# Four mixer layers on one core: softmax weights normalised on GpSimd before their transposes, and in the second layer GpSimd also makes low halves and ends rotations

## Chip, cores, metric

One core of one Trainium2 chip runs the whole program in one launch. The metric is the device time of one execution, in microseconds (us). The engines of the core are PE (TensorE, matmuls and transposes through the array; PEld is its weight load), DVE (VectorE), ACT (ScalarE), POOL (GpSimd) and SP (SyncE, which issues nearly all DMAs). PSUM is what PE writes to; DVE and ACT read and write it too.

## What is computed

A block with retention, mLSTM and a feed-forward part (`first_block`), and behind it four layers, whose mixers are dense attention, windowed attention with sinks, a long convolution, and dense attention again. The first and the fourth (8 heads, queries of 128 plus 64 rotated dimensions, 256 context keys and 512 own keys):

```python
def dense_attend(q, k, v, scale):
    s = jnp.einsum('bqhd,bkhd->bhqk', q, k).astype(jnp.float32) * scale
    p = jax.nn.softmax(s, axis=-1).astype(v.dtype)
    return jnp.einsum('bhqk,bkhd->bqhd', p, v)
```

The second has 16 query heads on 4 key heads of 64 dimensions; each query block of 128 sees up to three key blocks around it and the 256 context keys, and a sink, one learned score per head that enters the softmax and has no value row:

```python
def sink_attend(scores, values, sink_l):
    sink_col = jnp.broadcast_to(sink_l[None, :, :, None, None], scores[0].shape[:-1] + (1,))
    p = jax.nn.softmax(jnp.concatenate(scores + [sink_col], axis=-1), axis=-1)
...
```

Each attention output is multiplied by `silu(gate)` and goes through an output matrix. The third mixer needs filters `h @ f_w3` times an exponential decay for its convolution, and the kernel makes them early, beside the feed-forward part.

## The kernel before

All arithmetic is float32. To use PE's fast float32 format, every factor of a large product is split: the high half is the value rounded to that format (ACT, a copy), the low half what the rounding left (DVE, value minus high half). `split` (lines 396 to 398) does it. A product is three matmuls per 128 rows of depth, high by high, high by low and low by high (`mac`, lines 441 to 443). PE therefore has most of the work.

Weights come by DMA as `raw` tiles of 128x1024 (four buffers) and are split into `whi` and `wlo` (three of each, `wslot`) by `wm`, or into tiles that are held longer by `wheld` (`P` or `b` tiles). The stages are written as Python generators, and `mix` and `weave` interleave their steps, so that projections of the next heads lie between the attention steps of the present ones. From that the build makes one fixed list of instructions for each engine, and each engine works off its list in order; nothing overtakes.

Dense attention (`mla`): `prep` makes queries, keys and values of a pair of heads; its rotated query parts go through `rope64` (four ACT copies of 32 partitions in `swap32`, then line 1356 times cosine, 1357 times sine, 1358 the sum, all DVE) and `stacks`, which puts high and low half of 64 rows above each other. `stageA` makes the scores of 128 queries in PSUM (lines 1581 to 1583 and `mac`), and `softmax` makes the weights `P`: the largest score of each row (line 1380, DVE), times minus the scale (1382, DVE), the exponential with its row sum (1385, ACT), and 1 over the sum into a column of `rd` (1389, DVE). `P` stays unnormalised. `stageB` turns each block of 128 keys of the four (context: two) `P` tiles round on PE (`transposed`, line 1395), splits them out of PSUM, and multiplies with V. Only at the end it normalises: `over_columns` (line 1373) spreads the `rd` columns over all partitions by one PE transpose each, the gate `g` is multiplied with that (1605) and with the output (1606).

Windowed attention (`swa`): a unit is 128 queries of one key head with its four query heads; there are 24, of 256, 512 or 640 keys. `stageA` of one unit is mixed with `stageB` of the one before (`attend`). `softmax` gets the sink: the row maximum is held against it (1384), the sink's exponential (1387, ACT) is added to the sum (1388, DVE). In `stageB`, V is laid out as high half (64 columns) and low half (64 columns) of one stationary tile, `v[:, g]`, so that line 1739 gives two partial outputs on 128 partitions, and line 1738 or 1741 adds high half by low weights on 64 of them. Then `over_columns` again, ACT moves that to SBUF (1744), DVE multiplies (1745), adds the two halves (1749) and gates (1752).

Filters (`filter_head`, `filter_unit`): the hidden activations stand as high half (64 rows) over low half (64 rows) in `self.fh`; line 1873 multiplies 128 rows, line 1874 the upper 64 rows with the low halves of the filter weights. This is done 48 times.

Each normalisation of activations takes the power -0.5 of its sums on POOL (line 245, tile `rs`), which is spread by `over_columns` too. Otherwise POOL has little to do outside the third layer (lines 1995, 1996).

Of the kernel before, what the change touches and what calls it, by code (L numbers as in the profile page):

```python
# [19 lines left out]
N = 512  # L20
# [234 lines left out]
class Kern:  # L255
    def __init__(self, tc, I, coff, dbg=None):
        self.tc, self.nc, self.I, self.coff = tc, tc.nc, I, coff
        self.dbg = dbg or {}
        self.st = ExitStack()

# [135 lines left out]
    def split(self, dst, src):  # L396
        self.nc.scalar.copy(dst.hi, src)  # L397
        self.nc.vector.tensor_tensor(dst.lo, src, dst.hi.bitcast(F32), ALU.subtract)  # L398
# [12 lines left out]
    def wm(self, W, r0, kt, c0, n=128):  # L411

        t = self.wslot(kt, n)
        self.split(t, self.wload(W, r0, kt, c0, n))
        return [t[:, k, :] for k in range(kt)]

    def wheld(self, W, c0, slot, r0=0, kt=KT):
# [6 lines left out]
        for k in range(0, kt, per):  # L424
# [3 lines left out]
            self.split(t, raw[:, k:k + n, :])  # L428
# [932 lines left out]
    def stacks(self, r, n, d0, d1):  # L1361

        nc = self.nc
        nc.scalar.copy(d0[0:64, :], r[0:64, :])
        nc.vector.tensor_tensor(d0[64:128, :], r[0:64, :], d0[0:64, :].bitcast(F32), ALU.subtract)
        nc.scalar.copy(d1[64:128, :], r[64:128, :])
        nc.vector.tensor_tensor(d1[0:64, :], r[64:128, :], d1[64:128, :].bitcast(F32), ALU.subtract)
# [8 lines left out]
    def softmax(self, S, P, rd, scale, sink=None):  # L1376

        nc = self.nc
        s = self.sp.tile([128, 8], F32, tag="sm", name="sm")
        nc.vector.tensor_reduce(s[:, 0:1], S, AX.X, ALU.max)  # L1380
        if sink is None:
            nc.vector.tensor_scalar(s[:, 1:2], s[:, 0:1], -scale, None, ALU.mult)  # L1382
        else:
            nc.vector.tensor_scalar(s[:, 1:2], s[:, 0:1], -scale, sink[1], ALU.mult, ALU.min)
        nc.scalar.activation(P, S, AF.Exp, bias=s[:, 1:2], scale=scale, accum_out=s[:, 2:3])  # L1385
        if sink is not None:
            nc.scalar.activation(s[:, 3:4], sink[0], AF.Exp, bias=s[:, 1:2])
            nc.vector.tensor_tensor(s[:, 2:3], s[:, 2:3], s[:, 3:4], ALU.add)
        nc.vector.reciprocal(rd, s[:, 2:3])
# [716 lines left out]
```

## Time and profile before

| | |
|---|---|
| median of 3 runs | 2917.35 us (2915.61 to 2918.12) |
| the profiled execution | 2918.76 us |
| its span, first to last instruction | 2917.0 us |
| PE busy (matmuls) | 2787.1 us, 96% |
| DVE / ACT / POOL busy | 1814.9 (62%) / 1334.4 (46%) / 128.8 us (4%) |
| PE clock granted, mean | 0.982 of full speed |

PE's busy share counts a matmul from its start to a modelled end, and consecutive ones overlap, so the distance from one start to the next is the better measure of what a matmul takes. DVE is at 50 to 80% in most stretches. The stages follow one another: the first block to about 1295 us (the filters from 653 to 1005), the first layer's attention to about 1510, the second layer's from 1650 to 1990, the third layer to about 2500, the fourth layer's attention from 2678 to 2845.

### The profile page before, as it was taken

How to read it: one execution, taken by the hardware profiler on the slowest of the kernel's cores; microseconds unless marked ns; L12 is line 12 of the kernel's file. 1: busy time of each engine (PE TensorE's matmuls, PEld its weight loads, DVE VectorE, ACT ScalarE, POOL GpSimd, SP SyncE). 2: the span in 40 equal slices, each digit the busy share in tenths (PEclk: the TensorE clock that was granted, in tenths of full speed). 3: DMA queues.
4: the chain of work that ended last, by engine and by line, in shares of the span. 5: the costliest groups of instructions: out<-in, count | busy, mean ns of one | idle time of the engine just before them, and what ended most of it. 6: DMA issues, size and time to landing. Idle time of an engine off the chain costs nothing. (4 is left out here: it accounts for less than half of the span.)

```text
span 2917.0 us, 44103 instructions
## 1 busy us (share of the span) xinstructions
PE 2787.1 (96%) x17106; PEld 2364.2 (81%) x17106; DVE 1814.9 (62%) x3775; ACT 1334.4 (46%) x2610; POOL 128.8 (4%) x158
## 2 busy tenths in 40 slices
PE   7999999999999999999999999989999998999998
PEld 4888878887777787888889877778888886887887
DVE  6665455555655556246768577788576777754774
ACT  4344344346455433345555566675332223544553
POOL 1000000000000000000000000000021122000000
PEclk8999999999999999999999999999999999999998
DMA  7233232544555536321234241123132226432122
GB/s 264 86 111 123 73 101 84 168 154 141 164 158 163 170 112 209 108 67 44 68 93 156 64 131 42 35 71 117 62 95 84 84 80 195 130 97 63 56 82 69
DMA packets 365830, 318.98 MB, mean 109 GB/s; under 512 B 17511, under 2 KB 326517, under 8 KB 365620
## 3 DMA queue, kind: packets, MB, share of 16 engines
q1 hardware_dynamic: 365204, 315.99, 35.2%
q8 instruction: 134, 2.20, 0.3%
q14 instruction: 76, 0.62, 0.1%
q0 software_dynamic: 416, 0.17, 0.0%
HBM read 273.90 MB, written 42.21 MB: 108 GB/s over the span
## 5 line engine op out<-in xcount | busy, mean ns | idle before, releaser
L441 PE MATMUL mm<-b,whi 128*128 128x512 f32 (+1 forms) x2548 | 895.8, 352 | 4.7 <-ACT whi L397 2.5
L443 PE MATMUL mm<-b,wlo 128*128 128x512 f32 (+1 forms) x2548 | 887.3, 348 | 1.2 <-DVE wlo L398 1.1
L442 PE MATMUL mm<-b,whi 128*128 128x512 f32 (+1 forms) x2548 | 887.6, 348 | 0.0
L441 PEld LDWEIGHTS mm<-b,whi 128*128 128x128 f32 x2548 | 486.1, 191 | 74.4 <-issue 5.8
L443 PEld LDWEIGHTS mm<-b,wlo 128*128 128x128 f32 x2548 | 486.1, 191 | 62.0 <-DVE wlo L398 2.3
L442 PEld LDWEIGHTS mm<-b,whi 128*128 128x128 f32 x2548 | 486.5, 191 | 60.2 <-issue 0.8
L398 DVE TENSOR_TENSOR wlo<-raw,whi 128x1024 fp32r<-128x1024 f32 (+3 forms) x286 | 292.0, 1023 | 239.7 <-ACT whi L397 224.1
L397 ACT CAST whi<-raw 128x1024 fp32r<-128x1024 f32 (+3 forms) x286 | 252.3, 885 | 397.1 <-PE mm L442 253.9
L443 PE MATMUL mm<-b 128*128 128x256 f32 (+1 forms) x628 | 189.4, 302 | 0.5 <-DVE b L398 0.3
L1385 ACT ACTIVATE P<-mm,sm 128x768 f32<-128x768 f32 (+3 forms) x176 | 127.9, 727 | 116.6 <-DVE sm L1382 68.4
L441 PE MATMUL mm<-b 128*128 128x256 f32 (+1 forms) x500 | 158.2, 318 | 8.4 <-ACT P L1385 4.6
L441 PE MATMUL mm<-b,P 128*128 128x256 f32 x560 | 161.8, 289 | 4.0 <-ACT b L575 2.8
L442 PE MATMUL mm<-b,P 128*128 128x256 f32 x560 | 160.4, 286 | 0.9 <-DVE b L576 0.8
L442 PE MATMUL mm<-b 128*128 128x256 f32 (+1 forms) x500 | 153.0, 307 | 0.4 <-DVE b L398 0.3
L1380 DVE TENSOR_REDUCE sm<-mm 128x1 f32<-128x768 f32 (+3 forms) x176 | 128.6, 733 | 39.7 <-PE mm L1583 23.8
L245 POOL TENSOR_TENSOR rs<-rs,mhalf 128x2 f32<-128x2 f32 (+1 forms) x44 | 42.3, 962 | 2427.2 <-DVE rs L244 2279.8
L398 DVE TENSOR_TENSOR t<-mm,t 128x512 fp32r<-128x512 f32 (+1 forms) x208 | 136.5, 663 | 15.3 <-ACT t L397 14.1
L397 ACT CAST t<-mm 128x512 fp32r<-128x512 f32 (+1 forms) x208 | 116.0, 569 | 54.8 <-PE mm L1395 51.6
L235 DVE TENSOR_TENSOR t<-t 128x256 f32<-128x256 f32 (+1 forms) x216 | 92.5, 441 | 71.9 <-ACT t L231 69.4
L1395 PE MATMUL mm<-ct,P 128*128 128x128 f32 x768 | 122.8, 276 | 13.0 <-ACT P L1385 8.2
L231 ACT ACTIVATE t<-b 128x256 f32<-128x256 f32 (+1 forms) x252 | 100.7, 431 | 67.7 <-DVE b L1101 40.9
L443 PEld LDWEIGHTS mm<-b 128*128 128x128 f32 x628 | 120.6, 192 | 5.6 <-DVE b L398 1.3
(351 smaller groups left out, 5129.7 us busy)
## 6 DMA issues: line engine op xcount, KB each, us to landing
raw<-in_w_mod_dram SPq DMA_DIRECT2D x96, 512.0 KB, 4.4
raw<-in_w_ada_dram SPq DMA_DIRECT2D x48, 512.0 KB, 3.9
raw<-in_w_in_dram SPq DMA_DIRECT2D x48, 512.0 KB, 4.0
raw<-in_w_ffn_in_dram SPq DMA_DIRECT2D x44, 512.0 KB, 4.1
raw<-in_c_w_in_dram SPq DMA_DIRECT2D x32, 512.0 KB, 4.3
raw<-in_a_w_in_dram SPq DMA_DIRECT2D x28, 512.0 KB, 4.1
ks<-t SPq DMA_DIRECT2D x48, 256.0 KB, 2.8
raw<-ks SPq DMA_DIRECT2D x24, 512.0 KB, 3.3
```

Of the source, the lines that this page charges most:

```text
L231: self.k.nc.scalar.activation(sq, x, AF.Square)
L235: self.k.nc.vector.tensor_tensor(self.acc, self.acc, sq, ALU.add)
L245: nc.gpsimd.tensor_tensor(s[:, 4:4 + nt], s[:, :nt], self.k.mhalf[:, :nt], ALU.pow)
L397: self.nc.scalar.copy(dst.hi, src)
L398: self.nc.vector.tensor_tensor(dst.lo, src, dst.hi.bitcast(F32), ALU.subtract)
L441: nc.tensor.matmul(ps, l.hi, r.hi, start=start and i == 0, stop=False)
L442: nc.tensor.matmul(ps, l.hi, r.lo, start=False, stop=False)
L443: nc.tensor.matmul(ps, l.lo, r.hi, start=False, stop=stop and i == n - 1)
L1380: nc.vector.tensor_reduce(s[:, 0:1], S, AX.X, ALU.max)
L1385: nc.scalar.activation(P, S, AF.Exp, bias=s[:, 1:2], scale=scale, accum_out=s[:, 2:3])
L1395: self.nc.tensor.transpose(ps[:, 128 * i:128 * i + 128], b, self.ident)
```

## The change

The scale now goes into the queries when they are split. `softmax` takes the negated maximum in one DVE instruction, the exponential, 1 over the sum, and then POOL multiplies the `P` tile by it in place, before the transposes. With that the `over_columns` of `rd`, the multiplication of `g` (1605), and lines 1744 and 1745 go. In the second layer the sink is copied by ACT into the PSUM column behind the scores, so that maximum, exponential and sum take it in, and lines 1384, 1387, 1388 go; ACT copies the lower half of the output (64 partitions) to SBUF before the halves are added; the factor 0.5 moves to the gating; the low weights meet all 128 columns of `v[:, g]`, always behind the high ones. In the second layer (`self.low = nc.gpsimd`) the low halves of weights and the last two steps of a rotation go to POOL. In the filters the second matmul takes all 128 rows, with zeros (POOL memset, 8 times) under the low weights.

```diff
+    def split(self, dst, src, scale=None, low=None):
+        nc = self.nc
+        if scale is None:
+            nc.scalar.copy(dst.hi, src)
+            (low or nc.vector).tensor_tensor(dst.lo, src, dst.hi.bitcast(F32), ALU.subtract)
+        else:
+            nc.scalar.activation(dst.hi, src, AF.Copy, scale=scale)
+            nc.vector.scalar_tensor_tensor(dst.lo, src, scale, dst.hi.bitcast(F32), ALU.mult, ALU.subtract)
...
-        self.split(t, self.wload(W, r0, kt, c0, n))
+        self.split(t, self.wload(W, r0, kt, c0, n), low=self.low)
...
+        low = self.low or nc.vector
         nc.vector.tensor_tensor(a, ps, self.cs["ac"], ALU.mult)
-        nc.vector.tensor_tensor(sw, sw, self.cs["as"], ALU.mult)
-        nc.vector.tensor_tensor(a, a, sw, ALU.add)
+        low.tensor_tensor(sw, sw, self.cs["as"], ALU.mult)
+        low.tensor_tensor(a, a, sw, ALU.add)
...
-    def softmax(self, S, P, rd, scale, sink=None):
+    def softmax(self, S, P, keep):
...
+        s = self.sp.tile([128, 4], F32, tag="sm", name="sm")
+        nc.vector.tensor_reduce(s[:, 0:1], S, AX.X, ALU.max, negate=True)
+        nc.scalar.activation(P, S, AF.Exp, bias=s[:, 0:1], accum_out=s[:, 1:2])
+        nc.vector.reciprocal(s[:, 2:3], s[:, 1:2])
+        nc.gpsimd.tensor_scalar(P[:, :keep], P[:, :keep], s[:, 2:3], None, ALU.mult)
...
-            rd = o["rd", i]
-            nc.vector.tensor_tensor(g, self.over_columns([rd[:, x:x + 1] for x in range(n // 128)], 128), g, ALU.mult)
             nc.vector.tensor_tensor(g, out, g, ALU.mult)
...
+                nc.scalar.copy(ps[:, 768:769], self.sink[:, h:h + 1])
...
-                P = self.P(nb + 256)
-                h = 4 * g + v
-                self.softmax(ps[:, 512 - nb:768], P, rd[:, v:v + 1], scale, (self.sink[:, h:h + 1], nsink[:, h:h + 1]))
+                P = self.P(nb + 257)
+                self.softmax(ps[:, 512 - nb:769], P, nb + 256)
...
-                    last = z == nb + LS - 1
-                    if last:
-                        nc.tensor.matmul(out[:64, :], v[:, g, 0], p.lo, start=False, stop=False)
-                    nc.tensor.matmul(out, v[:, g], p.hi, start=z == LS, stop=last)
-                    if not last:
-                        nc.tensor.matmul(out[:64, :], v[:, g, 0], p.lo, start=False, stop=False)
+                    nc.tensor.matmul(out, v[:, g], p.hi, start=z == LS, stop=False)
+                    nc.tensor.matmul(out, v[:, g], p.lo, start=False, stop=z == nb + LS - 1)
...
-            nc.scalar.activation(rb, self.over_columns([rd[:, x:x + 1] for x in range(4)], 128), AF.Copy, scale=0.5)
-            nc.vector.tensor_tensor(rb, out, rb, ALU.mult)
+            nc.scalar.copy(rb[64:128, :], out[64:128, :])
...
+            nc.gpsimd.memset(l[64:128, :].bitcast(F32), 0.0)
...
-                        nc.tensor.matmul(ps, x[0:64, :], l, start=False, stop=True)
+                        nc.tensor.matmul(ps, x, l, start=False, stop=True)
```

What moves in the engines' lists, at two places. First PE's list in the first layer, where the first unit's weights `P` are turned round (line 1395 before, 1393 now; `mm2` are score tiles, `mm_11970` and `mm_11976` a gate projection). Before:

```order
L1583 MATMUL mm2_11908<-b_10189,b_11555 128x512
L1395 MATMUL mm_11928<-ct_98,P_11868 128x128
L1395 MATMUL mm_11928<-ct_98,P_11885 128x128
L441 MATMUL mm_11970<-b_11243,whi_11962 128x512
L442 MATMUL mm_11970<-b_11244,whi_11962 128x512
L1395 MATMUL mm_11928<-ct_98,P_11902 128x128
L441 MATMUL mm2_11938<-b_11767,b_11641 128x256
```

Now:

```order
L1393 MATMUL mm_11935<-ct_98,P_11892 128x128
L447 MATMUL mm_11976<-b_11251,whi_11968 128x512
L447 MATMUL mm2_11944<-b_11775,b_11649 128x256
L448 MATMUL mm2_11944<-b_11775,b_11649 128x256
L449 MATMUL mm2_11944<-b_11775,b_11650 128x256
L1580 MATMUL mm2_11944<-b_10198,b_11564 128x256
L1581 MATMUL mm2_11944<-b_10198,b_11564 128x256
L447 MATMUL mm2_11944<-b_11764,b_11649 128x512
L448 MATMUL mm2_11944<-b_11765,b_11649 128x512
L449 MATMUL mm2_11944<-b_11764,b_11650 128x512
L1580 MATMUL mm2_11944<-b_10196,b_11564 128x512
L1393 MATMUL mm_11935<-ct_98,P_11909 128x128
```

Between the second and the third tile's transposes there were 2 matmuls and are now 10: the next score tile went ahead of the third transpose.

Second, POOL's list where the first layer ends and the second begins. Before, it holds only the powers of the normalisations there (`rs`):

```order
L245 TENSOR_TENSOR rs_15009<-rs_15009,mhalf_114 128x2
L245 TENSOR_TENSOR rs_15181<-rs_15181,mhalf_114 128x2
L245 TENSOR_TENSOR rs_15347<-rs_15347,mhalf_114 128x2
L245 TENSOR_TENSOR rs_15548<-rs_15548,mhalf_114 128x2
L245 TENSOR_TENSOR rs_20114<-rs_20114,mhalf_114 128x2
```

Now, from the power that was `rs_15009`:

```order
L245 TENSOR_TENSOR rs_14921<-rs_14921,mhalf_114 128x2
L401 TENSOR_TENSOR wlo_15245<-raw_15246,whi_15244 128x1024
L401 TENSOR_TENSOR wlo_15644<-raw_15645,whi_15643 128x1024
L401 TENSOR_TENSOR P_15227<-raw_15224,P_15226 128x512
L401 TENSOR_TENSOR wlo_15650<-raw_15651,whi_15649 128x1024
L401 TENSOR_TENSOR P_15231<-raw_15224,P_15230 128x512
L401 TENSOR_TENSOR P_15237<-raw_15234,P_15236 128x512
L245 TENSOR_TENSOR rs_15093<-rs_15093,mhalf_114 128x2
L401 TENSOR_TENSOR P_15241<-raw_15234,P_15240 128x512
L245 TENSOR_TENSOR rs_15257<-rs_15257,mhalf_114 128x2
L245 TENSOR_TENSOR rs_15458<-rs_15458,mhalf_114 128x2
L1364 TENSOR_TENSOR t_15592<-t_15592,b_15220 128x512
```

Six low halves of the second layer's weights now stand ahead of the power `rs_15093`, and 176 multiplications of `P` (line 1387) and 20 rotation steps (1364, 1365) are added further along, among the low halves that follow.

## Rows read from the trace of the kernel before

**Rows 1.** Stages: us, busy (count) of PE, PEld, DVE, ACT, POOL, then clock, DMA.

```profile
640.00:1005.00 365.00, 365.00 (x1702) 276.04 (x1701) 202.32 (x298) 192.38 (x260) 0.00 (x0) 1.00 0.51 158
1300.00:1510.00 210.00, 201.94 (x1231) 173.92 (x1230) 144.11 (x324) 115.01 (x250) 0.00 (x0) 0.98 0.21 63
1650.00:1990.00 340.00, 309.61 (x1980) 259.00 (x1979) 261.53 (x713) 217.11 (x538) 0.00 (x0) 0.97 0.23 70
2678.00:2845.00 167.00, 162.43 (x926) 137.36 (x927) 115.36 (x226) 95.22 (x188) 0.00 (x0) 0.98 0.21 64
```

**Rows 2.** Groups by line, whole span: busy us, mean ns | idle before, releaser.

```profile
L1373 PE MATMUL mm<-ct,rd 128*128 128x128 f32 x176 | 28.6, 279 | 0.0
...
L1874 PEld LDWEIGHTS mm<-b 64*128 64x128 f32 x48 | 9.1, 190 | 14.6 <-issue 14.6
```

**Rows 3.** Timeline of PE at 1537 us: start, duration, line.

```profile
1537.45 0.60 PE L1373 MATMUL mm<-ct,rd 128*128 128x128 f32 x4
1537.81 0.36 PE L441 MATMUL mm<-b 128*128 128x256 f32 x1
```

**Rows 4.** Timeline of PE at 653 us, in a filter.

```profile
653.29 0.39 PE L443 MATMUL mm<-b,wlo 128*128 128x512 f32 x1
653.52 0.40 PE L1873 MATMUL mm<-b 128*128 128x512 f32 x1
653.85 0.50 PE L1874 MATMUL mm<-b 64*128 64x512 f32 x1
654.28 0.50 PE L1873 MATMUL mm<-b 128*128 128x512 f32 x1
```

**Rows 5.** Timeline of PE at 1891 us, in the second layer.

```profile
1891.43 0.47 PE L1739 MATMUL mm<-t,b 128*128 128x512 f32 x1
1891.75 0.40 PE L1741 MATMUL mm<-t,b 128*64 128x512 f32 x1
```

**Rows 6.** What PE and PEld waited for before line 1395: us, times.

```profile
  ACT P L1385: 21.8, 26
```

**Rows 7.** Timeline of DVE, ACT and PE at 1346 us: one softmax of 256 keys, and a maximum.

```profile
1343.34 0.95 DVE L1380 TENSOR_REDUCE sm<-mm 128x1 f32<-128x768 f32 x1
...
1346.00 0.15 DVE L1382 TENSOR_SCALAR sm<-sm 128x1 f32<-128x1 f32 x1
...
1346.19 0.47 ACT L1385 ACTIVATE P<-mm,sm 128x256 f32<-128x256 f32 x1 [0.38 <-DVE sm L1382]
...
1346.79 0.16 DVE L1389 RECIPROCAL rd<-sm 128x1 f32<-128x1 f32 x1 [0.63 <-ACT P L1385]
...
1346.81 0.44 PE L1395 MATMUL mm<-ct,P 128*128 128x128 f32 x2
```

**Rows 8.** Groups of POOL by line and shape, whole span.

```profile
L1995 POOL TENSOR_TENSOR t<-t 128x256 f32<-128x256 f32 x32 | 24.5, 766 | 298.0 <-DVE t L1994 255.4 <-issue 42.4
...
L245 POOL TENSOR_TENSOR rs<-rs,mhalf 128x2 f32<-128x2 f32 x31 | 25.0, 806 | 1807.4 <-DVE rs L244 1807.4
```

**Rows 9.** Groups of DVE by line and shape, 1660 to 2000 us.

```profile
L398 DVE TENSOR_TENSOR wlo<-raw,whi 128x1024 fp32r<-128x1024 f32 x17 | 20.7, 1218 | 6.6 <-ACT whi L397 6.4
L1384 DVE TENSOR_SCALAR sm<-sm,nsink 128x1 f32<-128x1 f32 x95 | 19.3, 207 | 1.1
L1745 DVE TENSOR_TENSOR t<-mm,t 128x512 f32<-128x512 f32 x24 | 16.6, 690 | 4.8 <-PE mm L1739 2.6 <-ACT t L1744 0.8 <-ACT P L1385 0.8
```

**Rows 10.** Waits of the weight loads, 1660 to 2000 us: us, times, longest.

```profile
PEld mm L1713 <- ACT P L1385: 14.7, 17, 2.0
PEld mm L1741 <- DVE t L398: 12.7, 17, 2.4
```

**Rows 11.** Timeline of DVE and POOL in the third layer, alone and together.

```profile
2134.63 0.69 DVE L398 TENSOR_TENSOR b<-t,P 128x512 fp32r<-128x512 f32 x1 [1.28 <-ACT P L397]
...
2144.73 0.74 POOL L1996 TENSOR_TENSOR t<-t 128x256 f32<-128x256 f32 x1
2144.76 1.25 DVE L398 TENSOR_TENSOR b<-t,P 128x512 fp32r<-128x512 f32 x1 [1.07 <-ACT P L397]
```

More of the change, by code (lines that the diff above doesn't have):

```diff
@@ L259, in __init__ @@
         self.st = ExitStack()
+        self.low = None
     def pool(self, name, bufs=1, space=None, st=None):
@@ L427, in wheld @@
             t = HL(hi.rearrange("p (k c) -> p k c", k=n), lo.rearrange("p (k c) -> p k c", k=n))
-            self.split(t, raw[:, k:k + n, :])
+            self.split(t, raw[:, k:k + n, :], low=self.low)
             out += [t[:, x, :] for x in range(n)]
@@ L1355, in rope64, with stacks @@
         a = self.t()
+        low = self.low or nc.vector
         nc.vector.tensor_tensor(a, ps, self.cs["ac"], ALU.mult)
-        nc.vector.tensor_tensor(sw, sw, self.cs["as"], ALU.mult)
-        nc.vector.tensor_tensor(a, a, sw, ALU.add)
-        return a
[L1361 to L1367, printed above, removed]
+        low.tensor_tensor(sw, sw, self.cs["as"], ALU.mult)
+        low.tensor_tensor(a, a, sw, ALU.add)
+        return a
+    def stacks(self, r, n, d0, d1, scale):
+        for d, h, l in ((d0, slice(0, 64), slice(64, 128)), (d1, slice(64, 128), slice(0, 64))):
+            self.split(HL(d[h, :], d[l, :]), r[h, :], scale)
     def over_columns(self, cols, m):
@@ L1560, in queries @@
                     q = self.bhl(n)
-                    self.split(q, self.proj([t[:, k, :] for k in range(4)], qn[i], n))
+                    self.split(q, self.proj([t[:, k, :] for k in range(4)], qn[i], n), scale)
                     o["q"].append(q)
@@ L1573, in stageA @@
             n = (N, NC)[i]
-            o["P", i], o["rd", i] = [], self.sp.tile([128, 4], F32, tag="rd", name="rd")
+            o["P", i] = []
             for qt in range(n // 128):
@@ L1585, in stageA @@
                 P = self.P(tot)
-                self.softmax(ps[:, off:off + tot], P, o["rd", i][:, qt:qt + 1], scale)
+                self.softmax(ps[:, off:off + tot], P, tot)
                 o["P", i].append(P)
@@ L1634, in swa @@
         self.axial()
-        nsink = self.c2.tile([128, 16], F32, name="nsink")
-        nc.vector.tensor_scalar(nsink, self.sink, -1.0, None, ALU.mult)
         V, ks, gq, gs = [], {}, {}, {}
@@ L1676, in f @@
                         gq[g, i] = [q[0][:, 0:256], q[0][:, 256:512], q[1][:, 0:256], q[1][:, 256:512]]
-                self.stacks(self.rope64(ps) if i == 0 else ps, ns[i], *gq[g, i][2 * u:2 * u + 2])
+                self.stacks(self.rope64(ps) if i == 0 else ps, ns[i], *gq[g, i][2 * u:2 * u + 2], scale)
             return f
@@ L1765, in attend @@
                 prev = units[n - 1] if n else None
-                yield from mix((stageA(*x), 4), (stageB(*prev), len(U[prev][2]) + 2) if prev else (None, 1))
+                yield from mix((stageA(*x), 4), (stageB(*prev), len(U[prev][1]) + 2) if prev else (None, 1))
+        self.low = nc.gpsimd
         weave((dense(0, WB - 2), 6))
@@ L1772, in swa @@
             weave((attend(units[6 * g:6 * g + 6 - (g == 3) * LT]), WS), (chain(dense(g + 1), gate(g + 1)) if g < 3 else end, 4 + (6 if g % 2 else 4) if g < 3 else ES), bg)
+        self.low = None
         return chain(attend(units[-LT:]), stageB(*units[-1])), 10 * LT + 5
@@ L1851, in filter_head @@
             nc.scalar.copy(w[64:128, :], w[0:64, :].bitcast(F32))
-            ws.append((w, l[0:64, :]))
+            nc.gpsimd.memset(l[64:128, :].bitcast(F32), 0.0)
+            ws.append((w, l))
         return dl, ws
```

30 lines of the change are left out of this document (8 added, 22 removed).

## The prediction

> **What bounds the kernel now.** I read the busy time by stages first, to see whether one engine fills them. It does: PE has all of 365 us where the filters are made, 202 of 210 in the first layer's attention, 162 of 167 in the fourth's, at nearly the full clock; in the second layer's attention it has 310 of 340, and DVE 262 [rows 1]. So time that is taken from PE's own list is saved nearly whole, and what happens on DVE, ACT or POOL costs only where PE stands and waits for it. The second view is the distance between starts on PE's timeline, since that tells what a matmul really takes. The third is what PE stood waiting for ahead of the transposes, because there the change puts a new step: 26 times, 21.8 us in all, it waited for the exponential [rows 6]. There the chain of a softmax lies open: maximum, small product, exponential, and the transposes start 0.15 us after the exponential ended (1346.19 + 0.47 against 1346.81), while 1 over the sum is still being made beside them [rows 7].
>
> The sum is made against the profiled execution, 2918.76 us, whose span is 2917.0; it stands 1.4 us above the median of the runs, 2917.35.
>
> **Removed from PE: the spreading of the sums.** 176 transposes [rows 2]. Four of them hold PE for 0.36 us (1537.45 to 1537.81) [rows 3]. There are 40 groups of four (8 + 8 heads over 512 queries, 24 units) and 8 of two: 40 x 0.36 + 8 x 0.18 = 15.8 us, all in stages that PE fills. **-16.** If a wait comes in their place they are worth less; that is counted below.
>
> **Removed from PE: the half-height matmul in the filters.** A 512-column matmul follows its like after 0.23 us (653.29 to 653.52). The one on 64 rows starts 0.33 after the one before it, and what follows it 0.43 later [rows 4]. On 128 rows both should be 0.23: 0.10 + 0.20 = 0.30, 48 times, **-14**. The weight load of that line stands idle for 14.6 us with nothing to wait for [rows 2], the same amount by another view. The zeros cost 8 fills on POOL, which has nothing to do in that stage [rows 1]. The Trainium skill speaks against this term: TensorE: Matmul & The Clock Gate, section "Why this matters for your kernels", says that a single matmul with few rows takes the same time as one with 128, by which nothing would be gained. The rows differ from it by 0.1 to 0.2 us, and I go by the rows.
>
> **Removed from PE: the half-width one in the second layer.** The 64-column line 1741 starts 0.32 us behind line 1739 [rows 5], 0.09 more than 0.23. Of 88 such pairs I take half to pay it, since others have something between them: **-4**, bounds 0 and -8.
>
> **Added: POOL between exponential and transposes.** No row shows a POOL product of a tile by one number per row. Bounds for 768 columns: 0.95 us, what DVE takes for a one-input pass [rows 7], and 2.3, three times the two-input POOL operation of 256 columns (0.77) [rows 8]. I take 1.3, nearer to the first because there is one input; for 256 columns by the same proportion 0.3 to 0.77, taken as 0.5. Added to each tile's way are that, 1 over the sum (0.16) and a hand-over of about 0.1 (an estimate from the 0.15 above); taken off is the small product (0.15). Net: the scale and 0.1, so 0.6 us for 256 columns and 1.4 for 768. The 26 waits, in all three attention stages, become longer by about 1.0 each, 26; tiles with little lead start to wait, +4; against that the list for PE now holds 10 instead of 2 matmuls ahead of the third tile's transposes, as the order shows for the first layer, -3. **+27**, bounds 10 and 62 (0.4 and 2.4 us, 26 times). The other 150 tiles have other matmuls ahead of their transposes and are taken at nothing; without that cover each would cost its 0.6 to 1.4. GPSIMD Engine Reference of the Trainium skill, section "Engine selection", calls POOL about twice as slow as DVE with two inputs and roughly at line rate with one; by that the term would lie in the lower half of the bounds.
>
> **Moved off DVE in the second layer.** DVE gives up 20.7 (17 low halves of weights), 19.3 and 16.6 us [rows 9], with smaller ones more than a fifth of its 262 [rows 1]. ACT trades the sink's exponential for a copy of one column, and one copy of 128 partitions for one of 64: nothing. PE's weight loads waited there 14.7 us for an exponential to give its score bank back and 12.7 for DVE's low halves of turned weights [rows 10]. A bit less than half of the two goes: **-12**, bounds 0 and -27.
>
> **Queued on POOL.** Six low halves now stand ahead of a power that PE needs at the end of the first layer, as the order shows; before, a power took 0.81 us and nothing stood ahead of it [rows 8]. A low half of 1024 columns takes between 1.22 us, DVE's time [rows 9], and 3.1, four times 0.77 [rows 8]. The first ones can be done early; two that become ready late hold the power for some 3 us. **+3**, bounds 0 and 12. The rotations wait for POOL too, but their keys and queries are needed a unit later.
>
> The sum is -16 - 14 - 4 + 27 - 12 + 3 = -16: 2902.8 for the profiled execution, **2901 us** as a median. Its own range, with half of the two large bounds used, is 2888 to 2911.
>
> **Rivals.**
> *The second layer was DVE's.* DVE has 262 of 340 us there and PE's 30 idle ones lie in that stage [rows 1]. If the whole 27 us of waits go and the scale takes 0.95, so that its term is 17: -16 - 14 - 4 + 17 - 27 + 3 = -41, 2876. Against it: the new step is in the same chain. Chance 0.15.
> *POOL is slow and collides with DVE (slower).* DVE's operation on two SBUF tiles takes 0.69 us alone and 1.25 beside a POOL operation [rows 11]. If the scale takes 2.3 us for 768 and is held up by half a microsecond like that, each of the 26 waits grows by some 2.2: 57, with the 4 of the others 61, and DVE's gain of 12 is eaten by its own delays: -16 - 14 - 4 + 61 + 3 = +30, 2946; half the collisions give 2930. It decides from 1.6 us of net delay per wait on. SBUF — State Buffer of the Trainium skill, section "Who interferes with whom", gives the mechanism: the two engines share one pair of ports, and a POOL operation that reads SBUF and a DVE operation with two SBUF inputs exclude each other for a whole instruction. The trace agrees, with 1.25 against 0.69. Against this rival: DVE's softmax work reads PSUM, one SBUF input at most. Chance 0.16.
> *POOL's list is the new order.* If low halves of weights that wait for a slot hold up the scales behind them in half of the 24 units by 1 us, and the power by 4 more: 16 less gain, 2901 + 13 to 16, so 2915. Chance 0.10.
> *The filter's step stays.* If the 0.10 and 0.20 us come from something else than the 64 rows, 14 less: 2915. For it stands the skill's rule, against it both rows 4 and the idle load. Chance 0.06.
>
> **The numbers.** Forecast 0.53, the rivals as given. About 0.2%, 6 us, is what a measurement of this kernel can tell from no change. Faster by that: 0.53 + 0.15 = 0.68; within it: 0.10 + 0.06 = 0.16; slower: 0.16. The range 2880 to 2926 leaves out the far half of the first and most of the second rival, under 0.2 together.
>
> **What would show it.** In the changed profile the filter's second matmul should follow after 0.23 us and its load have no idle time; the spreading of `rd` should be gone. The scale of 768 columns should take 1.0 to 1.6 us on POOL. The transposes should wait for POOL instead of ACT, some 26 to 40 times and about 45 us in all; over 70 us would prove the slower rival. DVE should fall below 200 us in the second layer's attention and that stage become shorter; if it keeps its length, the relief was worth nothing. The fourth layer's attention, which has only the scale and the missing transposes, should stay as long as it is.

## The result, and the profile after

The changed kernel takes **2953.99 us** (median of 4 runs, 2952.83 to 2955.46), the kernel before beside it 2916.48 (2913.54 to 2918.12): ratio 1.013, 95% interval 1.0112 to 1.0148. It is slower, by 37.5 us; the forecast was 2901. The profiled execution took 2955.46 us, its span is 2953.7.

To see where the 36.7 us between the two spans arose, I cut both traces at the same events: an attention runs from the first row maximum (`sm`, DVE) of its layer to the start of the last transpose of a `P` tile (PE).

| stretch, us | before | after | difference |
|---|---|---|---|
| up to the first layer's attention (filters in it) | 1301.7 | 1287.1 | -14.6 |
| first layer's attention | 228.6 | 246.7 | +18.2 |
| between it and the second layer's | 122.5 | 130.5 | +8.0 |
| second layer's attention | 335.1 | 346.6 | +11.5 |
| up to the fourth layer's | 688.0 | 689.2 | +1.2 |
| fourth layer's attention | 173.1 | 185.5 | +12.4 |
| rest | 68.1 | 68.1 | 0.0 |

How well such lengths repeat: in the six kernels below whose first attention has the old code it took 228.5 to 229.0 us; the fourth has the old code in the same six and took 171.4 to 173.0, so the kernel before lies at the upper end there. The long stretches vary more between executions of the same code: the one up to the first attention by up to 9 us, the one from the second to the fourth by up to 7.

The stages of the changed kernel, cut there (us, busy (count) of PE, PEld, DVE, ACT, POOL, then clock, DMA share, GB/s; they answer to [rows 1]):

```profile
640.00:990.00 350.00, 348.54 (x1703) 276.97 (x1702) 200.50 (x297) 192.10 (x260) 3.12 (x6) 1.00 0.53 165
...
1287.00:1534.00 247.00, 223.12 (x1339) 193.57 (x1338) 142.16 (x273) 123.71 (x269) 86.23 (x48) 0.95 0.20 61
1534.00:1664.00 130.00, 121.62 (x933) 118.04 (x932) 81.47 (x176) 67.16 (x151) 31.97 (x22) 0.97 0.33 104
1664.00:2011.00 347.00, 301.68 (x1855) 252.31 (x1854) 206.44 (x464) 208.84 (x532) 195.86 (x126) 0.96 0.23 68
```

The kernel before, its first and second attention cut the same way:

```profile
1302.00:1530.00 228.00, 219.94 (x1376) 191.64 (x1375) 151.10 (x335) 123.23 (x267) 0.00 (x0) 0.99 0.21 65
...
1653.00:1988.00 335.00, 304.61 (x1944) 254.59 (x1942) 258.52 (x707) 214.56 (x532) 0.00 (x0) 0.97 0.24 71
```

The filter stage is shorter, as forecast. In the second layer's attention DVE lost a fifth of its work and the stage still grew: DVE did not bound it. In the first layer's attention PE has now 24 idle us in 247, where it had 8 in 228, and its granted clock is 0.95 where it was 0.99 over the old stage: it ran at 1.2 instead of 2.4 GHz for 23.9 us, before for 6.8. Over the three attentions it was at 1.2 GHz for 62.2 us, before for 30.7; against full speed half of such time is lost.

The groups of POOL by line and shape (x count | busy us, mean ns | idle before; they answer to [rows 8]):

```profile
L1387 POOL TENSOR_SCALAR P<-P,sm 128x768 f32<-128x768 f32 x64 | 143.0, 2236 | 317.5 <-DVE sm L1386 307.8 <-PE mm L1393 9.7
...
L1387 POOL TENSOR_SCALAR P<-P,sm 128x256 f32<-128x256 f32 x48 | 47.3, 991 | 41.1 <-DVE sm L1386 38.0 <-DMA od<-t 2.5 <-PE mm L1393 0.6
L401 POOL TENSOR_TENSOR wlo<-raw,whi 128x1024 fp32r<-128x1024 f32 x18 | 43.1, 2399 | 16.1 <-ACT whi L400 16.1
```

The scale of 768 columns takes 2.24 us, where 1.3 was taken. What PE and PEld waited for before the transposes, together, in the whole span (us, times; it answers to [rows 6]):

```profile
  POOL P L1387: 122.8, 85
```

And the view of waits for PE alone (us, times, longest):

```profile
PE mm L1393 <- POOL P L1387: 55.6, 41, 4.4
```

The first view counts a matmul and its weight load apart; it was so in [rows 6] too. PE's own part of those 21.8 us, in the kernel before:

```profile
  ACT P L1385: 8.2, 8
```

So PE stands there 41 times instead of 8, and for 47 us more. One of these waits, on the timeline of all engines (start, duration; in brackets the idle time before it):

```profile
1331.46 3.10 POOL L1387 TENSOR_SCALAR P<-P,sm 128x768 f32<-128x768 f32 x2 [2.07 <-DVE sm L1386]
...
1332.05 0.38 PE L1393 MATMUL mm<-ct,P 128*128 128x128 f32 x2
...
1334.62 0.44 PE L1393 MATMUL mm<-ct,P 128*128 128x128 f32 x2 [2.08 <-POOL P L1387]
```

Two scales, of 768 and of 256 columns, run one behind the other until 1334.56; the transposes start 0.06 us later, and PE stood 2.08 us.

### The profile page after: what moved, and what is told of

Read it like the earlier page. It is cut to its first block, busy times and chain, and to the rows that moved or that the text cites. A ratio compares the mean times of both kernels' runs of the same rounds, so it can differ in the third digit from the quotient of the medians.

```text
span 2953.7 us, 43876 instructions
## 1 busy us (share of the span) xinstructions
PE 2769.3 (94%) x16930; PEld 2361.6 (80%) x16930; DVE 1742.2 (59%) x3408; ACT 1330.7 (45%) x2610; POOL 513.7 (17%) x388
## 5 line engine op out<-in xcount | busy, mean ns | idle before, releaser
L401 DVE TENSOR_TENSOR wlo<-raw,whi 128x1024 fp32r<-128x1024 f32 (+3 forms) x268 | 270.7, 1012 | 233.8 <-ACT whi L400 220.9
L1387 POOL TENSOR_SCALAR P<-P,sm 128x768 f32<-128x768 f32 (+3 forms) x176 | 303.1, 1730 | 444.9 <-DVE sm L1386 416.1
L449 PE MATMUL mm<-b 128*128 128x256 f32 (+1 forms) x628 | 193.0, 308 | 0.5 <-DVE b L401 0.3
L1393 PE MATMUL mm<-ct,P 128*128 128x128 f32 x768 | 133.1, 287 | 58.5 <-POOL P L1387 55.6
L1384 DVE TENSOR_REDUCE sm<-mm 128x1 f32<-128x768 f32 (+4 forms) x176 | 128.6, 735 | 79.1 <-PE mm L1581 36.1
L1385 ACT ACTIVATE P<-mm,sm 128x768 f32<-128x768 f32 (+4 forms) x176 | 128.4, 730 | 87.1 <-DVE sm L1384 85.8
L1393 PEld LDWEIGHTS mm<-ct,P 128*128 128x128 f32 x768 | 96.6, 146 | 87.4 <-POOL P L1387 67.2
L447 PE MATMUL mm<-b 128*128 128x256 f32 (+1 forms) x500 | 159.7, 321 | 5.0 <-ACT b L400 3.7
L448 PE MATMUL mm<-b 128*128 128x256 f32 (+1 forms) x500 | 156.8, 314 | 0.0
```

The lines of the kernel that those rows point to most:

```text
L401: (low or nc.vector).tensor_tensor(dst.lo, src, dst.hi.bitcast(F32), ALU.subtract)
L447: nc.tensor.matmul(ps, l.hi, r.hi, start=start and i == 0, stop=False)
L448: nc.tensor.matmul(ps, l.hi, r.lo, start=False, stop=False)
L449: nc.tensor.matmul(ps, l.lo, r.hi, start=False, stop=stop and i == n - 1)
L1384: nc.vector.tensor_reduce(s[:, 0:1], S, AX.X, ALU.max, negate=True)
L1385: nc.scalar.activation(P, S, AF.Exp, bias=s[:, 0:1], accum_out=s[:, 1:2])
```

## The experiments

All numbers below are against the kernel before on the same chip. The stretches are cut as above, from the profiled execution of each.

| kernel | median us | ratio, 95% interval | att. 1 | between | att. 2 | att. 4 |
|---|---|---|---|---|---|---|
| before | 2916.5 to 2919.5 | | 228.6 | 122.5 | 335.1 | 173.1 |
| after | 2953.99 | 1.013, 1.0112 to 1.0148 | 246.7 | 130.5 | 346.6 | 185.5 |
| filter_only | 2902.53 | 0.9956, 0.9940 to 0.9973 | 228.8 | 122.4 | 335.0 | 171.4 |
| full_only | 2920.80 | 1.0008, 0.9997 to 1.0018 | 228.8 | 122.5 | 336.4 | 171.9 |
| late_pool | 2901.59 | 0.9943, 0.9928 to 0.9957 | 224.4 | 130.7 | 330.6 | 168.2 |
| late_dve | 2885.90 | 0.9889, 0.9873 to 0.9906 | 224.9 | 122.5 | 325.6 | 168.4 |
| scale_dve | 2908.56 | 0.9967, 0.9954 to 0.9980 | 225.3 | 130.6 | 337.7 | 170.4 |
| low_dve | 2934.26 | 1.0053, 1.0038 to 1.0068 | 247.8 | 124.3 | 330.4 | 183.7 |
| both_dve | 2897.03 | 0.9935, 0.9920 to 0.9950 | 227.5 | 124.1 | 330.4 | 170.5 |
| scale_split | 2900.17 | 0.9950, 0.9936 to 0.9965 | 231.8 | 122.9 | 333.2 | 171.9 |
| scale_tt | 2922.92 | 1.0009, 0.9999 to 1.0019 | 233.6 | 129.2 | 337.0 | 178.6 |
| scale_out | 2869.97 | 0.9832, 0.9811 to 0.9853 | 218.7 | 122.7 | 316.5 | 165.9 |
| low_only | 2937.16 | 1.0071, 1.0054 to 1.0087 | 228.6 | 130.6 | 345.3 | 173.0 |
| low_quarters | 2930.64 | 1.0038, 1.0025 to 1.0052 | 228.5 | 126.7 | 341.4 | 171.5 |
| low_weights | 2938.33 | 1.0053, 1.0035 to 1.0071 | 229.0 | 128.7 | 348.5 | 171.5 |
| low_turns | 2926.08 | 1.0026, 1.0015 to 1.0037 | 228.7 | 126.1 | 340.6 | 171.9 |

### Two small terms alone: filter_only, full_only

```diff
-            ws.append((w, l[0:64, :]))
+            nc.gpsimd.memset(l[64:128, :].bitcast(F32), 0.0)
+            ws.append((w, l))
...
-                        nc.tensor.matmul(ps, x[0:64, :], l, start=False, stop=True)
+                        nc.tensor.matmul(ps, x, l, start=False, stop=True)
```

> The kernel before with one part of the change alone: the filters' second matmul on all 128 rows, with zeros under the low weights. If the 14.6 us that the stages of the changed kernel show up to the first attention are this matmul's, 2917 - 14 to 15 = 2902 to 2903, and from the first attention on every stage as before. If part of them came from another edit, less: 2905 to 2917.

Measured 2902.53, ratio 0.9956, and the gain lies ahead of the first attention. In the changed kernel a filter's two matmuls now follow each other like any others (PE's timeline; it answers to [rows 4]):

```profile
653.60 0.39 PE L1867 MATMUL mm<-b 128*128 128x512 f32 x1
653.83 0.39 PE L1868 MATMUL mm<-b 128*128 128x512 f32 x1
654.07 0.39 PE L1867 MATMUL mm<-b 128*128 128x512 f32 x1
```

0.23 us from start to start, where the 64-row one cost 0.33 and 0.43. The term of -14 stands: 48 times 0.30 is 14.4. (The interval of the ratio alone leaves 8 to 17.5 us.)

```diff
-                    if last:
-                        nc.tensor.matmul(out[:64, :], v[:, g, 0], p.lo, start=False, stop=False)
-                    nc.tensor.matmul(out, v[:, g], p.hi, start=z == LS, stop=last)
-                    if not last:
-                        nc.tensor.matmul(out[:64, :], v[:, g, 0], p.lo, start=False, stop=False)
+                    nc.tensor.matmul(out, v[:, g], p.hi, start=z == LS, stop=False)
+                    nc.tensor.matmul(out, v[:, g], p.lo, start=False, stop=z == nb + LS - 1)
```

> The kernel before with one part alone: the low weights of the second layer meet all 128 columns of the stationary tile, always behind the high ones. The prediction gave -4, bounds 0 and -8: 2913, range 2909 to 2917, all of it in the second layer's attention (335 to 331).

Nothing was gained: the interval holds 1, and the second attention is 1.3 us longer. The term had no ground, since the distance that it was to shorten did not shrink: where the two matmuls follow each other directly, the second starts 0.31 us behind the first on 128 columns (median of 58), and 0.32 on 64 columns in the kernel before (median of 49). So the 0.09 us over the usual 0.23 do not come from the width; from what else is not shown.

### Which part loses: late_pool, late_dve, scale_dve, low_dve

late_pool takes the changed kernel and normalises behind the product with V, as before:

```diff
-        nc.vector.reciprocal(s[:, 2:3], s[:, 1:2])
-        nc.gpsimd.tensor_scalar(P[:, :keep], P[:, :keep], s[:, 2:3], None, ALU.mult)
+        nc.vector.reciprocal(rd, s[:, 1:2])
...
+            rd = o["rd", i]
+            nc.vector.tensor_tensor(g, self.over_columns([rd[:, x:x + 1] for x in range(n // 128)], 128), g, ALU.mult)
             nc.vector.tensor_tensor(g, out, g, ALU.mult)
...
-            nc.scalar.copy(rb[64:128, :], out[64:128, :])
+            nc.scalar.activation(rb, self.over_columns([rd[:, x:x + 1] for x in range(4)], 128), AF.Copy, scale=0.5)
+            nc.vector.tensor_tensor(rb, out, rb, ALU.mult)
```

> The changed kernel with the normalisation put back behind the product with V (rd columns spread by transposes, no POOL step between exponential and transposes); everything else of the change stays, low halves and rotations of the second layer on POOL too. Stage by stage the changed kernel lost 18.2 us in the first layer's attention, 8.0 between it and the second layer's, 11.5 in the second's and 12.4 in the fourth's, and won 14.6 in the filters. Theory A (the loss is the POOL step ahead of the transposes): the first and fourth attentions return to their old length (228 and 173 us), the 8.0 between stays, the second layer's attention comes to 335 or under; in all 2954 - 18 - 12 - 12 to 16 = 2908 to 2912. Theory B (the loss is POOL's queue, low halves and rotations ahead of what PE needs): only the first and fourth come back, the second layer's stage stays near 346; about 2922.

late_dve has that and leaves out `self.low = nc.gpsimd`:

> As the run with the late normalisation, and low halves and rotations of the second layer on DVE as before; what is left of the change is the filters' full-height matmul, the full-width one with low weights, the sink as a score column, the negated maximum and the scale in the queries. Both theories: the 8.0 us between the first and second attention go too; 2917 - 14.6 (filters) - 4 (full width) - up to 5 (three DVE steps of a softmax gone) = 2893 to 2899. If moving the low halves to POOL helped the second layer by itself, its attention is longer here than in the other late run, by up to 12 us, and the total nearer 2900.

scale_dve has the changed kernel's scale on DVE (`nc.vector.tensor_scalar` in line 1387):

> The changed kernel with the multiplication of P by 1/sum on DVE instead of POOL, same place in the chain. Theory A1 (the loss is POOL's slowness: 2.24 us for 768 columns): one DVE pass of 768 columns takes 0.95 us, so each of the 44 waits of the weight loads ahead of the transposes (67 us) shrinks by some 1.0 to 1.3 us; 2954 - 35 to 45 = 2909 to 2919, DVE's extra 176 passes (some 130 us) cost up to 10 of it. Theory A2 (the loss is one more link in the chain, whoever does it): little is won, 2940 or over. Theory A3 (DVE is too full in the second layer): first and fourth attention come back by 10 us each, the second gets longer than 346.

low_dve is the changed kernel without `self.low = nc.gpsimd`:

> The changed kernel with low halves and rotations of the second layer on DVE as before; the scale stays on POOL. Theory A (the step ahead of the transposes): the 8.0 us between the first and the second attention go, since no low half stands ahead of a power on POOL; the second attention changes by less than 5 either way; 2944 to 2950. Theory B (POOL's queue): the second attention also falls, by 10 or more, and the waits of the transposes for POOL in it (24 us of the weight loads) fall to under 12; 2930 to 2938.

The results separate two losses. Without the POOL scale the first and fourth attention fall from 246.7 and 185.5 to 224.4 and 168.2 (late_pool), 4 to 5 us below the kernel before; with the scale on DVE they are at 225.3 and 170.4. So the link in the chain costs far less where its engine is quick, and A1 holds: POOL's slowness is what the dense layers lost. The second loss belongs to `self.low`: the 8 us between the attentions are there in the three runs so far that have low halves and rotations on POOL (130.5 to 130.7), with or without a scale there; they are gone in late_dve, and all but 1.8 in low_dve. The second attention also gets shorter once they are back on DVE, by 5 us with the late normalisation (330.6 to 325.6), by 16 with the scale on POOL (346.6 to 330.4), where both stand in one list. That is what theory B had for low_dve in its total and its second attention; its sign for the waits was met in part, since the weight loads' wait for the scale in that stage fell from 24.0 to 16.2 us, not under 12. Both late runs came out 6 to 7 us under the lower ends of what I expected: I had missed that the shorter softmax is itself worth something (the table of terms below has it).

### The price of the step: both_dve, scale_split, scale_tt, scale_out

both_dve has the scale, the low halves and the rotations on DVE:

> The changed kernel with nothing on POOL in the attention layers: the scale, the low halves and the rotations all on DVE. Against the version with late normalisation on DVE (2885.9) it has one step more ahead of the transposes, some 80 to 130 us more of DVE work, and 176 transposes less on PE (18 us). Theory A1 (POOL's slowness was the loss): first and fourth attention at 225 and 170, no 8 us between, second attention 328 to 335; 2890 to 2899. Theory A2 (the link itself costs, once DVE is also full): the second attention over 340, 2905 or more.

2897.03, as A1 has it. DVE needs 0.62 us for what POOL does in 2.24 (DVE's group of 768 columns, 64 times):

```profile
L1387 DVE TENSOR_SCALAR P<-P,sm 128x768 f32<-128x768 f32 x64 | 39.6, 619 | 1.9
```

scale_split shares the columns of a tile (low halves on DVE):

```diff
+        f = 128 * ((keep // 128 + 1) // 2)
+        nc.vector.tensor_scalar(P[:, :f], P[:, :f], s[:, 2:3], None, ALU.mult)
+        nc.gpsimd.tensor_scalar(P[:, f:keep], P[:, f:keep], s[:, 2:3], None, ALU.mult)
```

> As the version with nothing on POOL, but the scale is shared: DVE takes the first half of the columns (128-blocks rounded up), POOL the rest at the same time. By the rows POOL then needs 0.36 + 384 x 0.00245 = 1.3 us for the half of a 768-column tile, DVE some 0.55. If the transposes of the first three blocks wait for DVE's half alone, the chain is as short as on DVE, with half of DVE's load: 2888 to 2896. If they wait for both halves, each of some 44 waits is 0.35 to 0.5 us longer than with DVE alone, and the first and fourth attention grow by 5 to 9 and 3 to 5: 2900 to 2912.

Its median lies where the second case begins, and in its profiled execution, 10.8 us above that median, each attention is a little longer than with DVE alone. POOL took 1.42 us for its 384 columns, and PE and PEld waited 28.1 us for POOL's half and 3.5 for DVE's. Sharing gave nothing against DVE alone; whether it lost something the overlapping intervals do not tell.

scale_tt writes the changed kernel's scale as a product of two tiles:

```diff
-        nc.gpsimd.tensor_scalar(P[:, :keep], P[:, :keep], s[:, 2:3], None, ALU.mult)
+        nc.gpsimd.tensor_tensor(P[:, :keep], P[:, :keep], s[:, 2:3].to_broadcast([128, keep]), ALU.mult)
```

> The changed kernel with POOL's multiplication of P written as a product of two tiles, the column of 1/sum read with stride zero, instead of a product with one number per row. By POOL's two-input rows (256 columns 0.77 us, 1024 columns 2.40) 768 columns would take 1.86 us instead of 2.24. If the form sets the price, each of the 44 waits is 0.3 to 0.4 us shorter and the total 2936 to 2944; if POOL's price is the pass over 768 columns whatever the form, 2951 to 2957; if the two inputs now collide with DVE, over 2957.

It won more than any case had, 31 us by the medians: the same product on the same engine takes a third less. POOL's group of 768 columns in that run:

```profile
L1387 POOL TENSOR_TENSOR P<-P,sm 128x768 f32<-128x768 f32 x64 | 95.2, 1489 | 347.6 <-DVE sm L1386 341.5 <-PE mm L1393 6.1
```

0.75 us less per 768 columns, and the waits of PE and PEld before the transposes fall from 122.8 us to

```profile
  POOL P L1387: 71.3, 74
```

PE's own part of them falls from 55.6 us to

```profile
PE mm L1393 <- POOL P L1387: 29.8, 31, 3.4
```

That is 26 us less, where the two profiled executions lie 27.5 us apart; the time at 1.2 GHz falls with it, in the three attentions from 62.2 us to 37.5. By the traces PE, ACT, DVE and POOL have the same lists of instructions in both, and only the form and the duration of this step differ, so the loss in the attentions goes with that duration. The shorter form even holds DVE up more: DVE's two-tile operations beside the scale were over their kind's median by 24.5 us in all, beside the slower form by 6.9.

scale_out omits line 1387 (low halves on DVE):

> The version with nothing on POOL in the attention layers, and the multiplication of P by 1/sum left out altogether, so the attention outputs are not normalised: a price for the step, not a kernel to use. If the step ahead of the transposes is what the version with everything on DVE (2897) loses against its 18 us of saved transposes, this one is at the late normalisation's 2886 less 18 = 2866 to 2872, with 44 waits gone. If the 18 us of transposes were covered anyway, 2878 to 2886.

2869.97, in the first case's range. The three attentions take 701.1 us together, against 718.9 with late normalisation (late_dve), 728.4 with a DVE step (both_dve) and 761.9 with the POOL step (low_dve). Normalising costs 18 us late, 27 on DVE and 61 on POOL. The 18 are the whole late normalisation, with its steps on ACT and DVE; the 176 transposes alone were forecast at 16. Every step that I tried in its place cost more. Of the 27, waits ahead of the transposes are little: PE's own for `P` are 9.5 us with the step on DVE and 7.9 without any. What grew is the time at 1.2 GHz in the three attentions, from 17.9 us to 58.0, of which half is lost; it is 6.8 with late normalisation and 51.7 with the POOL step. What lowers the clock with the step on DVE is not shown.

### Low halves and rotations on POOL: low_only, low_quarters, low_weights, low_turns

low_only is the kernel before with `self.low = nc.gpsimd` in the second layer and nothing else:

> The kernel before with one part alone: in the second layer the low halves of weights and the last two steps of a rotation on POOL. The prediction gave this -12 for the relief of DVE and +3 for POOL's queue: 2908. Theory B1 (POOL's 2.4 us for a low half of 1024 columns, where DVE has 1.2, makes weights and rotated keys late, and the power on POOL stands behind six of them): +8 between the first and second attention, 0 to +6 in the second, 2925 to 2931. Theory B2 (POOL's low halves only hurt because the scales stand beside them in the list): +8 between, the second attention shorter by some 5, 2920.

Slower by 20 us, more than B1 had: +8.1 between the attentions, +10.2 in the second, the first and fourth unmoved. The changed kernel's trace tells what happens between them. Its timeline at 1583 us, POOL and DVE (start, duration):

```profile
1583.01 2.53 POOL L401 TENSOR_TENSOR wlo<-raw,whi 128x1024 fp32r<-128x1024 f32 x1
...
1583.26 2.55 DVE L1315 TENSOR_TENSOR b<-b,t 128x256 f32<-128x256 f32 x1
...
1585.74 0.41 DVE L235 TENSOR_TENSOR t<-t 128x256 f32<-128x256 f32 x1
```

A DVE addition of two SBUF tiles that takes 0.42 us stands until POOL's low half is over. The Trainium skill has this on the page SBUF — State Buffer, section "Who interferes with whom": a DVE instruction with two SBUF inputs contends with a GpSimd instruction that reads SBUF, and the port pair that they share is an exclusive lock. The trace agrees, 2.55 us beside 2.53. ACT's next square comes after that, and PE waits for the sum of squares (waits of PE, 1534 to 1664 us):

```profile
PE mm L242 <- DVE t L235: 4.8, 2, 4.4
PE mm L1377 <- POOL rs L245: 2.1, 2, 1.1
```

The powers on POOL, which I had thought of, make PE wait 2.1 us here and 2.4 in the kernel before. Behind the 4.4 us of waiting PE's clock was granted at 1.2 GHz for 6.8 us, and a stretch that had the clock at 1.00 has 0.97. The wait and half of those 6.8 us make 7.8 of the 8.0 that the stretch lost.

To see whether POOL's lateness or this holding is the cause, low_quarters makes each low half in four pieces:

```diff
+        s = max(1, kt // 4)
+        for a in range(0, kt, s):
+            low.tensor_tensor(dst.lo[:, a:a + s, :], src[:, a:a + s, :], dst.hi[:, a:a + s, :].bitcast(F32), ALU.subtract)
```

> The run with only the low halves and rotations on POOL (2937 us), but each low half of weights is made in four pieces: 4 x 256 columns instead of 1024, 4 x 128 instead of 512. Theory C (while POOL works on two SBUF inputs, a DVE operation with two SBUF inputs stands until POOL's instruction is over: a 128x256 addition took 2.55 us instead of 0.42 beside a low half of 2.53): a piece is over after 0.8 us, so DVE is held for less, the 4.5 us wait of PE for the squares between the first and second attention falls under 2, that stretch from 130.6 to 124 to 127, the second attention from 345 to 337 to 342, in all 2920 to 2931. Theory D (POOL is late with the low halves, whatever DVE does): four pieces take 3.1 us instead of 2.4, so nothing is won, 2937 to 2945.

Theory C's side: POOL works longer (72 pieces of 0.80 us instead of 18 of 2.41), and still the stretch between falls by 3.9 us and the second attention by 3.9. By the trace, DVE's two-tile operations beside POOL were over their kind's median by 8.8 us in 7 cases between the attentions of low_only, by 5.4 in 15 here. PE's longest wait between the attentions fell from 4.5 us, not under 2:

```profile
PE mm L242 <- DVE t L235: 2.8, 2, 2.5
```

D falls as the only cause.

The last two take the parts of low_only apart (the edit against low_only):

```diff
-        low = self.low or nc.vector
+        low = nc.vector
```

(low_weights; low_turns instead drops `low=self.low` in `wm` and `wheld`.)

> The kernel before with the low halves of weights alone on POOL in the second layer, the rotations on DVE. The run with both lost 8.1 us between the first and second attention and 10.2 in the second. Theory C (the loss is DVE held by POOL's long two-input operations): the 26 low halves are 54 us of POOL against 26 us of rotations, and all of those that lie between the attentions; 130 to 131 between, the second attention 341 to 344, 2931 to 2935. Theory D (the loss in the second attention is turned keys and queries that come late, since two POOL steps take 2.6 us where two DVE steps take 1.4): the second attention within 2 us of 335, 2924 to 2927.

> The kernel before with the last two steps of a rotation alone on POOL in the second layer, the low halves on DVE. Theory C: between the attentions as before (122.5, +0 to 1), the second attention 337 to 339, 2919 to 2922. Theory D: the second attention 342 to 345, 2924 to 2927.

By the ratios weights alone cost 15 us, rotations alone 8, both together 21. Weights alone are far over D's 2924 to 2927, with a second attention of 348.5, longer even than C had it. Rotations alone, at 2926, are where D had them. The profiled execution took 10.9 us more than that median, but most of that lies in the two long stretches (1307.4 and 692.4 us, against 1301.7 and 688.0 before); its 126.1 between the attentions is 3.6 over the kernel before, where C had 0 to 1, and its second attention of 340.6 lies between C's and D's. So neither theory is enough: the weights carry the larger part, as C says, and the rotations cost more than C allows them.

## Why the prediction was wrong

By its own terms (us, in the order of its sum; measured from the stretches of two kernels that differ in that part):

| term | forecast | measured | by |
|---|---|---|---|
| spreading transposes | -16 | -17.8 | scale_out against late_dve, three attentions (with the ACT and DVE steps of the late normalisation) |
| filters | -14 | -14.6 | after against before, up to the first attention |
| full width | -4 | 0 | full_only |
| POOL between exponential and transposes | +27 | +60.8 | low_dve against scale_out: 29.1 + 13.9 + 17.8 |
| moved off DVE, queued on POOL | -12, +3 | +22.4 | after against low_dve: 6.2 between, 16.2 in the second attention |
| softmax with fewer steps | not a term (line 1384 is in the -12) | -17.9 | late_dve against before: 3.7 + 9.5 + 4.7 (full width in it) |

They add to +32.9 of the 36.7; what is left, 3.8, is spread over stretches at which these pairs differ by 1 to 2 us each. PE's list is not in the same order in the two kernels of such a pair, as it is in after and scale_tt; what that adds to a measured term is not known.

**What bounds the kernel** was read rightly: PE's list was shortened and gave back about what was forecast for the transposes and the filters. On the filters the rows were right against the rule that the prediction weighs them with.

**The failed step is the +27 for POOL between exponential and transposes.** The mechanism was named, a wait for POOL ahead of the transposes, and the size was wrong in two factors. The 768-column scale was taken as "1.3, nearer to the first because there is one input"; it took 2.24, next to the upper bound of 2.3. The argument from the number of inputs was false: the same product with two inputs takes 1.49. By GPSIMD Engine Reference of the Trainium skill, section "Engine selection", one input runs roughly at line rate; the runs differ, 2.24 us against DVE's 0.62. For the two-input low half its factor of two holds: 2.40 on POOL, 1.22 on DVE [rows 9]. Second, "the other 150 tiles ... are taken at nothing": PE stood before 41 transposes, not before 8 that waited in the old trace, and the row with 26 had counted PE and its weight load apart. The count would have failed with the right price too: in scale_tt the step takes 1.49 us, and PE still stood 31 times for 29.8 us. The clock added its part, which the prediction had not in its sum: of the 60.8 us, the time at 1.2 GHz in the three attentions is 51.7 us in low_dve and 17.9 in scale_out, so some 17 us are lost to it, part of it while PE stood anyway.

**What moved off DVE to POOL, in the -12, had the wrong sign.** DVE's busy time fell from 259 to 206 us between the same two events. But PE's waits for DVE did not fall with the work that moved: in the second attention they are 11.4 us in the kernel before and 17.1 in low_only, 10.7 in late_dve and 13.5 in late_pool. The engine that took the work holds DVE up while it does it, and needs twice as long. The mechanism stood in the prediction, with [rows 11], but was spent on the wrong operation: in the changed kernel's trace 84 two-tile operations of DVE ran beside the scale and were over their kind's median by 6.9 us in all, while 30 ran beside low halves and rotations and were over it by 12.6. The -12 counted lines 1384 and 1745 too, which were not moved but removed; what they gave is in the -17.9 and -17.8.

**Queued on POOL, +3,** did not come as it was named: PE waited no longer for the powers (2.1 us there, 2.4 before). The same low halves cost 6 to 8 us in that stretch by holding DVE, which stays under the bound of 12, for another reason.

**Missing was a gain of some 18 us,** priced as 0.15 per tile and "nothing": a maximum that comes negated, the scale in the queries, the sink as a column of scores. late_dve has these, the filters and the full width, which gave nothing. Which of the three edits earns it was not tried apart. Much of it is clock: the time at 1.2 GHz in the three attentions is 6.8 us in late_dve and 30.7 in the kernel before, half of the difference is 12 us.

**The rivals.** The slower one came nearest: its 61 us for the waits are the 61 measured, its 2946 is 8 below the result. The agreement is in part luck. Its 61 are 26 waits that grow by 2.2 us, a collision in each, and 4 for others; the runs show 41 waits of PE and lost clock, and a scale of 768 columns takes 2.21 us as a median, whether a two-tile operation of DVE runs beside it or not; its total also leaves out the -17.9 and the +22.4, which nearly cancel. Of its two causes the slowness was the true one; the collision is real, in another place. Of the signs that the prediction named, "over 70 us would prove the slower rival" was met with 122.8, in the count that takes PE and its weight load apart; the fourth layer's attention, which was to "stay as long as it is", grew by 12.4. Two of the prediction's own sums do not come out: half of the two large bounds gives 2885 to 2924, not 2888 to 2911, and the rival with half the collisions 2935 or more, not 2930.

**What beats both kernels** is late_dve, 2885.90, ratio 0.9889 (0.9873 to 0.9906) to the kernel before: the late normalisation, nothing moved to POOL, and the rest of the change.

**Open** is how the 5 to 16 us that low halves and rotations on POOL cost within the second attention divide between held DVE operations, later weights, and scales behind them in POOL's list. For the 16, between low_dve and the changed kernel, the traces show a part: PE's own wait there for the scale grew from 12.0 to 19.2 us, and its time at 1.2 GHz from 17.6 to 28.0.

## What to carry to other kernels

A step that is put into a chain must be priced at the slow end of its bounds if no row shows that very form on that engine, and one short run of it alone costs less than the argument; here the same product on one engine took 2.24 or 1.49 us by how it was written. Before work is moved to an idle engine, ask which operations of the relieved one it will hold up meanwhile, and whether the relieved one was waited for at all. And where a row of waits counts an engine and its weight load, count the engine alone. Last, read the granted clock beside the waits: between the attentions 4.4 us of waiting were followed by 6.8 us at 1.2 GHz.

## What the runs showed of the hardware that was not expected

- POOL multiplies 128x768 by one number per row in 2.24 us, and by a broadcast column as a second tile in 1.49; DVE does the first in 0.62.
- Even the smallest DVE operation on two SBUF operands can stand beside POOL: in low_weights a sum of one column took 1.48 us, where most take 0.15. Its timeline, POOL and DVE:

```profile
1736.31 2.39 POOL L399 TENSOR_TENSOR wlo<-raw,whi 128x1024 fp32r<-128x1024 f32 x1 [17.22 <-ACT whi L398]
...
1737.24 1.48 DVE L1390 TENSOR_TENSOR sm<-sm 128x1 f32<-128x1 f32 x1 [0.91 <-ACT sm L1389]
```

- A DVE operation that reads PSUM was not touched: in the first attention of the changed kernel a row maximum of 768 columns took 0.96 us in the 16 cases that overlap a scale on POOL, and 0.95 in the 16 that do not.
- How much POOL holds DVE depends on the form of POOL's operation too. Of DVE's two-tile operations that started inside a scale, 17 of 59 took over 0.1 us more than their kind's median where POOL multiplied by one number per row (the changed kernel), and 32 of 35 where it multiplied two tiles (scale_tt).
